# Hybrid decoder layer on one core: where seven big SBUF tiles begin, and which of their columns the up and down products use

## The chip, the cores and the metric

The kernel runs on one core of one Trainium2 chip. The metric is the time of one execution on the device in microseconds (us). Before the change it is 1274.11 us, the median of three runs (1274.04 to 1275.34).

## The reference, cut to what matters

One layer of a decoder over 1024 tokens and 16 meta tokens, model width 1024: an input projection, a convolution branch and a banded attention branch, both projected back and merged by gates, an output projection with a layer norm, and a feed-forward block of width 2816. The parts that the change touches are the last ones:

```
mixed = jax.nn.sigmoid(g_attn) * y_attn + jax.nn.sigmoid(g_conv) * y_conv
h = layer_norm(DEEPNORM_ALPHA * h + mixed @ w_out, ln1_g, ln1_b)
up = causal_dwconv(h @ ffn_w_up, ffn_dw, ffn_dw_b)
u, g = jnp.split(up, 2, axis=-1)
f = (jax.nn.gelu(g, approximate=False) * u) @ ffn_w_down
return layer_norm(DEEPNORM_ALPHA * h + f, ln2_g, ln2_b)
```

## The kernel before, in words

**Numbers in halves.** Each float32 operand of a large product is split into a high and a low part of type fp32r. A product is the sum of three: high by high, high by low, low by high. So matmuls come in threes, and each has a stationary operand of 128 columns of its own (loaded by LDWEIGHTS) and a moving operand of 256 to 512 columns. The code names the first operand of `nc.tensor.matmul` (after the output) the stationary one, the second the moving one.

**Stages.** The input projection (`ps_z`, L295 to L300, from operands in RHC and RHO), attention between its tiles, the two branch projections (`ps_p`, from OA and OC), the output projection (`ps_w`, `out_rows`, stationary pieces of the mixed rows in RHC and RHO, moving weights in OA, RX, RW and two small tiles), then up and down.

**Up** (L1480, the loop over 22 chunks `c`). Up is done as a Strassen product: seven products in place of eight. For each chunk there are seven stationary weight sums, and each is multiplied with one of seven sums of the rows, in two sub-blocks: sub-block 0 has 258 columns, sub-block 1 has 256. A product on one sub-block is 12 matmuls (four pieces of the contraction, three matmuls each), so a chunk has 7 x 2 x 12 = 168 matmuls, and the stage 3696. `B_AT` says in which tile and from which column each of the 14 row sums lies; a sum takes 4 x 258 x 2 = 2064 columns or 4 x 256 x 2 = 2048 columns, the four high pieces first and then the four low ones. The weights come from a ring of ten places of 1024 columns (`RING`): four in RHO from column 0, four in small tiles that the page names `ws`, and two in RHO from column 6160. Seven places are used in each chunk, so the ring turns against the seven products.

**Down** (L1613, `down`). Also seven products, each over 11 pieces taken in six pairs, four output rows of banks: 7 x 11 x 4 x 3 = 924 matmuls of 512 columns. The stationary operand (the activations) lies at the places of `F_AT`, six in turn; the moving one (the weights) at those of `W_DN`, seven in turn.

**Order.** Nothing in the order of the engines' work hangs on a byte address: the instructions are put in order by priorities (`rank`) and by `after`, and the tiles are placed by pools that stack from the left or the right end of SBUF. The built program of the changed kernel has the same instructions in the same order on every engine, queue for queue, with the same semaphore waits but for one value on DVE; only the addresses differ.

**Places in bytes.** In the built program FA, RHC, RHO and OB begin at a byte whose residue modulo 256 is 192, and so do the small weight tiles (`wr`, `whi`, `wlo`, `ws`). OA begins at residue 0, RX, RW and the two tiles of `sums` at 64, OC at 128. A column has 4 bytes, so 64 columns make 256 bytes.

Of the kernel before, what the change touches and what calls it, by code (L numbers as in the profile page):

```python
# [23 lines left out]
F = mybir.dt.float32  # L24
# [5 lines left out]
P = 128  # L30
# [71 lines left out]
def tile_hybrid_layer(  # L102
# [41 lines left out]
    RHC = arena.tile([P, 8320], R, name="RHC")  # L144
    RHO = arena.tile([P, 8320], R, name="RHO")
# [756 lines left out]
    late = ctx.enter_context(tc.tile_pool(name="late", bufs=1, side="right", reuse_waits="tile"))  # L902

    OC = late.tile([P, 8320], R, name="OC")
    late.tile([P, 24], F, name="pad_c")
    oa_stack = ExitStack()
    oa_p = oa_stack.enter_context(tc.tile_pool(name="oa", bufs=1, side="left", reuse_waits="tile"))
    oa_p.tile([P, 8], F, name="pad_a")
    OA = oa_p.tile([P, 8320], R, name="OA")
    tmp_stack = ExitStack()  # L910
    tmp_p = tmp_stack.enter_context(tc.tile_pool(name="tmp", bufs=1, side="right", reuse_waits="tile"))
# [104 lines left out]
    tmp_stack.close()  # L1016
    rx_p = ctx.enter_context(tc.tile_pool(name="rx", bufs=1, side="right", reuse_waits="tile"))
    RX = rx_p.tile([P, 2064], R, name="RX")
    wo_stack = ExitStack()
    RW = wo_stack.enter_context(tc.tile_pool(name="rw", bufs=1, side="right", reuse_waits="tile")).tile(  # L1020
        [P, 2048], R, name="RW")
# [22 lines left out]
    def prep_wo(k, raw=None, behind=None):  # L1044
        if k < 4:
            hi, lo = OA[:, k * 2048:k * 2048 + 1024], OA[:, k * 2048 + 1024:k * 2048 + 2048]
        elif k < 6:
            hi, lo = ((RX, RW)[k - 4][:, x:x + 1024] for x in (0, 1024))
        else:
# [83 lines left out]
    def quadrant(sub, kk, h):  # L1133
# [1 line left out]
        return FA[:, h1_at(sub, i):h1_at(sub, i + 4)]  # L1135


    B_AT = [[(RHC, 6256), (RHO, 4096), (OA, 0), (OA, 2064), (OA, 4128), (OA, 6192), (RX, 0)],
            [(OC, 0), (OC, 2048), (OC, 4096), (OC, 6144), (RHC, 112), (RHC, 2160), (RHC, 4208)]]
    B11, B21, BT2, BT1, BT3, BT4, B22 = range(7)  # L1140

    def bsum(sub, q, hl):
        n = SUB[sub][1] - SUB[sub][0]
        t, o = B_AT[sub][q]
        return t[:, o + hl * 4 * n:o + (hl + 1) * 4 * n]
# [141 lines left out]

    RING = [RHO[:, i * 1024:(i + 1) * 1024] for i in range(4)]
    RING += [None] * 4
    RING += [RHO[:, 6160 + i * 1024:6160 + (i + 1) * 1024] for i in range(2)]  # L1290
    ring_next = [0]

    def wsplit(src):
# [253 lines left out]
    T1, T3, T4, T2 = (blk(td, 0, 2048, q * 512) for q in range(4))  # L1547
    S2, S3, S4, S1 = (blk(sd, 0, 2048, q * 512) for q in range(4))

    F_AT = [(RHC, 6256), (RX, 0), (RHC, 2160), (RHO, 0), (RHO, 2048), (RHO, 4096)]  # L1550
    W_DN = [(OC, 0), (OC, 2048), (OC, 4096), (OC, 6144), (RHC, 112), (RHC, 4208), (RHO, 6144)]

    RXFs = [RXF[:, 0:1024], RXF[:, 1024:2048]]
    FAs = [FA[:, i * 1024:(i + 1) * 1024] for i in range(6)]
# [7 lines left out]
    def operand(i, src, j, n, raws, places):  # L1562
        raw = raws[i % len(raws)]
        if raw is None:
            raw = wraw([P, D])
        raw = raw[:, :n * 512]
        ins = load(raw.rearrange("p (n c) -> p n c", c=512), src(j, n))
        after(ins, loads[-1] if loads else f_stores[-5])
        loads.append(ins)
        t, o = places[i % len(places)]  # L1570
        hi, lo = (t[:, o + x:o + x + n * 512] for x in (0, 1024))
        nc.scalar.copy(hi, raw)
        los.append(nc.vector.tensor_tensor(lo, raw, f32(hi), OP.subtract))
        if len(los) > 1:
            after(los[-1], evacs.pop() if evacs else los[-2])
        return hi, lo

    def down_operands():
# [4 lines left out]
        for i, (f, w, j, n) in enumerate(x):  # L1583
            yield (n,) + operand(i, f, j, n, F_RAW, F_AT) + operand(i, w, j, n, W_RAW, W_DN)

# [181 lines left out]
```

## Time and profile before

| what | before |
|---|---|
| median of the runs | 1274.11 us |
| span of the profiled execution, first to last instruction | 1273.1 us |
| TensorE matmul (PE) busy | 1261.4 us, 8546 records |
| VectorE (DVE) busy | 1084.0 us |
| ScalarE (ACT) busy | 587.9 us |
| DMA, mean over the span | 167 GB/s |

The profiled execution itself took 1273.1 us by its instructions; the run times are about 1 us longer, with what lies ahead of the first instruction and behind the last one. A record of a matmul in the profile is longer than the matmul's turn on the engine: matmuls are pipelined, and one starts while the one before it still drains. So the time that a matmul takes of the stage is read from the distance between starts, and for a group of rows of the timeline it is the start of the next row less the start of this one, divided by the count. The second column of such a row is the time to the end of its last record.

### The profile page before, as it was taken

How to read it: one execution, taken by the hardware profiler on the slowest of the kernel's cores; microseconds unless marked ns; L12 is line 12 of the kernel's file. 1: busy time of each engine (PE TensorE's matmuls, PEld its weight loads, DVE VectorE, ACT ScalarE, POOL GpSimd, SP SyncE). 2: the span in 40 equal slices, each digit the busy share in tenths (PEclk: the TensorE clock that was granted, in tenths of full speed). 3: DMA queues.
4: the chain of work that ended last, by engine and by line, in shares of the span. 5: the costliest groups of instructions: out<-in, count | busy, mean ns of one | idle time of the engine just before them, and what ended most of it. 6: DMA issues, size and time to landing. Idle time of an engine off the chain costs nothing.

```text
span 1273.1 us, 21682 instructions
## 1 busy us (share of the span) xinstructions
PE 1261.4 (99%) x8546; PEld 1189.6 (93%) x8546; DVE 1084.0 (85%) x1837; ACT 587.9 (46%) x1066; POOL 53.1 (4%) x28
## 2 busy tenths in 40 slices
PE   9999999999999999999999999999999999999997
PEld 8999999999999999788899999999999998888885
DVE  7899989999999577548899999988989876996697
ACT  7522254645573232344655455455554544444330
POOL 0000000010112231000000000000000000000000
PEclk9999999999999999999999999999999999999999
DMA  7294633332256564222145546454454567988722
GB/s 275 74 306 106 184 93 99 102 95 84 68 152 177 158 165 117 83 90 76 67 158 200 190 168 214 158 207 145 156 196 161 202 225 284 387 317 310 247 83 83
DMA packets 96152, 212.10 MB, mean 167 GB/s; under 512 B 10787, under 2 KB 35939, under 8 KB 95922
## 3 DMA queue, kind: packets, MB, share of 16 engines
q1 hardware_dynamic: 84282, 199.64, 47.2%
q10 hardware_dynamic: 11768, 11.08, 2.7%
q8 instruction: 67, 1.10, 0.4%
q14 instruction: 35, 0.29, 0.1%
HBM read 150.29 MB, written 62.70 MB: 167 GB/s over the span
## 4 chain that ended last, share of the span: by engine, by line
PE 96%; DMA 2%; DVE 1%; ACT 0%; issue 0%; SPq 0%; DVEq 0%; ACTq 0%
PE px L1480 15%; PE ps_x L1613 10%; PE py L1480 10%; PE ps_z L299 7%; PE ps_z L295 7%; PE ps_z L300 7%; PE ps_z L1613 7%; PE pz L1480 5%; PE pw L1480 5%; PE ps_p L299 2%; PE ps_p L300 2%; PE ps_p L295 2%; PE ps_w L300 2%; PE ps_w L295 2%; PE ps_w L299 2%; PE ps_z L511 2%
## 5 line engine op out<-in xcount | busy, mean ns | idle before, releaser
L663 DVE SCALAR_TENSOR_TENSOR FA<-cin,cols,FA 128x1026 f32<-128x1026 f32 x120 | 155.1, 1303 | 0.2
L295 PE MATMUL ps_z<-RHO,whi 128*128 128x384 f32 (+2 forms) x324 | 104.8, 323 | 0.0
L299 PE MATMUL ps_z<-RHC,whi 128*128 128x384 f32 (+2 forms) x324 | 104.7, 323 | 0.0
L299 PE MATMUL ps_z<-RHO,whi 128*128 128x384 f32 (+2 forms) x324 | 104.0, 321 | 0.0
L295 PE MATMUL ps_z<-RHC,whi 128*128 128x384 f32 (+2 forms) x324 | 103.9, 321 | 0.0
L300 PE MATMUL ps_z<-RHC,wlo 128*128 128x384 f32 (+2 forms) x324 | 103.6, 320 | 0.0
L300 PE MATMUL ps_z<-RHO,wlo 128*128 128x384 f32 (+2 forms) x324 | 103.2, 319 | 0.0
L1302 DVE TENSOR_TENSOR RHO<-wr,RHO 128x512 fp32r<-128x512 f32 x94 | 63.4, 683 | 9.8 <-ACT RHO L1301 9.8
L1301 ACT CAST RHO<-wr 128x512 fp32r<-128x512 f32 x94 | 56.6, 619 | 26.4 <-DVE wr L1319 10.1
L266 ACT CAST whi<-wr 128x1024 fp32r<-128x1024 f32 x37 | 38.9, 1052 | 56.8 <-PE ps_z L299 36.7
L295 PEld LDWEIGHTS ps_z<-RHO,whi 128*128 128x128 f32 x324 | 60.9, 188 | 0.5 <-issue 0.3
L299 PEld LDWEIGHTS ps_z<-RHC,whi 128*128 128x128 f32 x324 | 60.9, 188 | 0.4
L300 PEld LDWEIGHTS ps_z<-RHC,wlo 128*128 128x128 f32 x324 | 61.0, 188 | 0.2
L300 PEld LDWEIGHTS ps_z<-RHO,wlo 128*128 128x128 f32 x324 | 60.9, 188 | 0.1
L295 PEld LDWEIGHTS ps_z<-RHC,whi 128*128 128x128 f32 x324 | 60.8, 188 | 0.2
L299 PEld LDWEIGHTS ps_z<-RHO,whi 128*128 128x128 f32 x324 | 60.9, 188 | 0.1
L1319 DVE TENSOR_TENSOR wr<-wr 128x512 f32<-128x512 f32 x88 | 60.0, 682 | 0.2
L269 POOL TENSOR_TENSOR wlo<-wr,whi 128x1024 fp32r<-128x1024 f32 x17 | 41.3, 2431 | 187.5 <-ACT whi L266 177.7
L1492 ACT COPY FA<-px 128x514 f32<-128x514 f32 (+2 forms) x23 | 13.2, 572 | 76.4 <-PE px L1480 76.4
L670 ACT ACTIVATE FA<-ps_z,cols 128x386 f32<-128x386 f32 (+2 forms) x48 | 26.0, 541 | 47.5 <-PE ps_z L300 43.0
L1302 DVE TENSOR_TENSOR ws<-wr,ws 128x512 fp32r<-128x512 f32 x60 | 40.6, 684 | 5.4 <-ACT ws L1301 5.3
L1480 PE MATMUL px<-OA,RHO 128*128 128x258 f32 x324 | 43.1, 282 | 0.0
(467 smaller groups left out, 3583.9 us busy)
## 6 DMA issues: line engine op xcount, KB each, us to landing
wr<-in_w_up_dram SPq DMA_DIRECT2D x44, 512.0 KB, 4.3
wr<-in_w_z_dram SPq DMA_DIRECT2D x30, 512.0 KB, 3.7
fd<-FA SPq DMA_DIRECT2D x44, 256.0 KB, 2.5
OB<-in_w_down_dram SPq DMA_DIRECT2D x19, 512.0 KB, 6.1
qt<-qd SPq DMA_DIRECT2D x28, 256.0 KB, 3.8
td<-OB SPq DMA_DIRECT2D x12, 512.0 KB, 3.5
sums<-fd SPq DMA_DIRECT2D x12, 512.0 KB
sd<-sums SPq DMA_DIRECT2D x12, 512.0 KB, 2.9
```

The costliest lines, as they stand in the source:

```text
L266: ins = nc.scalar.copy(hi, raw)
L269: return (nc.vector if quick else nc.gpsimd).tensor_tensor(lo, raw, f32(hi), OP.subtract)
L295: ins = nc.tensor.matmul(ps, ah, bh, start=i == 0, stop=False)
L299: nc.tensor.matmul(ps, ah, bl, start=False, stop=False)
L300: last = nc.tensor.matmul(ps, al, bh, start=False, stop=i == n - 1)
L663: nc.vector.scalar_tensor_tensor(acc[c], cin[:, j:j + U], wc, acc[c], OP.mult, OP.add)
L670: nc.scalar.activation(t, ps, AF.Tanh, bias=bcol(14 + i), scale=0.5)
L1301: nc.scalar.copy(hi, src)
L1302: ins = nc.vector.tensor_tensor(lo, src, f32(hi), OP.subtract)
L1319: ins = nc.vector.tensor_tensor(*x)
L1480: ins = nc.tensor.matmul(o, x[:, ks], bmat(sub, q, hl, k), start=first and k + j == 0, stop=k == 3 and j == 2, skip_group_check=not first)
L1613: nc.tensor.matmul(banks[i], l[:, ts], r[:, ws], start=first and a and x + k == 0, stop=z and x == len(ops) - 1 and k == 2, skip_group_che ...
```

## The change

It moves where tiles begin, by the size of three filler tiles (one of them new), and moves the columns that some operands take within their tiles. `late`, `oa` and `rx` are pools; `pad_c`, `pad_a` and `pad_x` are never read or written.

```
     OC = late.tile([P, 8320], R, name="OC")
-    late.tile([P, 24], F, name="pad_c")
+    late.tile([P, 8], F, name="pad_c")
...
-    oa_p.tile([P, 8], F, name="pad_a")
+    oa_p.tile([P, 56], F, name="pad_a")
     OA = oa_p.tile([P, 8320], R, name="OA")
...
     RX = rx_p.tile([P, 2064], R, name="RX")
+    rx_p.tile([P, 48], F, name="pad_x")
...
-    B_AT = [[(RHC, 6256), (RHO, 4096), (OA, 0), (OA, 2064), (OA, 4128), (OA, 6192), (RX, 0)],
-            [(OC, 0), (OC, 2048), (OC, 4096), (OC, 6144), (RHC, 112), (RHC, 2160), (RHC, 4208)]]
+    B_AT = [[(RHC, 6208), (RHO, 4096), (OA, 0), (OA, 2064), (OA, 4128), (OA, 6208), (RX, 0)],
+            [(OC, 16), (OC, 2064), (OC, 4112), (OC, 6160), (RHC, 2064), (RHC, 16), (RHC, 4112)]]
     B11, B21, BT2, BT1, BT3, BT4, B22 = range(7)
...
-    RING += [RHO[:, 6160 + i * 1024:6160 + (i + 1) * 1024] for i in range(2)]
+    RING += [RHO[:, 6208 + i * 1024:6208 + (i + 1) * 1024] for i in range(2)]
...
-    F_AT = [(RHC, 6256), (RX, 0), (RHC, 2160), (RHO, 0), (RHO, 2048), (RHO, 4096)]
-    W_DN = [(OC, 0), (OC, 2048), (OC, 4096), (OC, 6144), (RHC, 112), (RHC, 4208), (RHO, 6144)]
+    F_AT = [(RHC, 6208), (RX, 0), (RHC, 0), (RHO, 0), (RHO, 2048), (RHO, 4096)]
+    W_DN = [(OC, 0), (OC, 2048), (OC, 4096), (OC, 6144), (RHC, 2048), (RHC, 4096), (RHO, 6144)]
```

In the built program of the changed kernel FA, RHC, RHO, OB, OA, OC and RX all begin at residue 192 (RW and the two tiles of `sums` too). The residues of the first bytes of the operands, before and after:

| operand | before | after |
|---|---|---|
| up, stationary: ring places | 192 (eight places), 0 (two) | 192 (all ten) |
| up, moving, sub-block 1 (256 columns) | 128 (all seven) | 0 (all seven) |
| up, moving, sub-block 0 (258 columns): B11, B21, BT2, BT1, BT3, BT4, B22 | 128, 192, 0, 64, 128, 192, 64 | 192, 192, 192, 0, 64, 192, 192 |
| down, stationary (`F_AT`) | 128, 64, 128, 192, 192, 192 | 192 (all six) |
| down, moving (`W_DN`) | 128 (six places), 192 (one) | 192 (all seven) |

In sub-block 0 each of the four pieces lies 258 columns behind the one before it, so its residue is 8 more, and the low pieces lie 32 further; this is the same before and after.

## Prediction

> **What bounds the kernel now.** I read the page first, then the time of each engine by stage (the windows), then the timeline of PE, row by row.
>
> ```profile
> span 1273.1 us, 21682 instructions
> PE 1261.4 (99%) x8546; PEld 1189.6 (93%) x8546; DVE 1084.0 (85%) x1837; ACT 587.9 (46%) x1066; POOL 53.1 (4%) x28
> PE 96%; DMA 2%; DVE 1%; ACT 0%; issue 0%; SPq 0%; DVEq 0%; ACTq 0%
> 634.00:1051.80 417.80, 417.80 (x3542) 417.80 (x3541) 377.78 (x604) 219.30 (x361) 0.00 (x0) 1.00 0.52 183
> 1051.80:1265.20 213.40, 213.32 (x926) 173.36 (x925) 169.68 (x239) 82.03 (x92) 0.00 (x0) 1.00 0.69 247
> ```
>
> The first three lines are from the page: PE is busy for 99% of the span, and 96% of the chain that ended last is PE. The last two are windows: the stretch, its length, then busy time and count of PE, weight load, DVE, ACT and POOL, granted clock, DMA share and GB/s. Nearly all of up (634 to 1051.8) and all of down (1051.8 to 1265.2) run without an idle PE at full granted clock. So the time of these 631 us is the number of matmuls times the distance between their starts, and that distance is what I looked at. In up it is 417.80 / 3542 = 118.0 ns on average. The change leaves all instructions, their order and their waits alone and changes addresses; whether it does anything is whether the distance between starts depends on addresses. It does, and the timeline of down shows it:
>
> ```profile
> 1057.31 5.66 PE L1613 MATMUL ps_z<-OC,RX 128*128 128x512 f32 x24
> 1062.80 5.60 PE L1613 MATMUL ps_z<-OC,RHC 128*128 128x512 f32 x24
> 1068.24 5.76 PE L1613 MATMUL ps_z<-OC,RHO 128*128 128x512 f32 x24
> 1073.84 5.76 PE L1613 MATMUL ps_z<-RHC,RHO 128*128 128x512 f32 x24
> 1079.44 2.93 PE L1613 MATMUL ps_z<-RHO,RHC 128*128 128x512 f32 x12
> ...
> 1190.33 5.64 PE L1613 MATMUL ps_x<-RHO 128*128 128x512 f32 x24
> 1195.81 8.56 PE L1613 MATMUL ps_x<-OC,RHO 128*128 128x512 f32 x36
> ```
>
> These are the same 24 matmuls of 512 columns each time, with no idle time between, and only the places differ. Let the **distance** be the residue of the moving operand less that of the stationary one, modulo 256 bytes. OC with RHC (column 2160) is 128 and 128, distance 0: 1068.24 - 1062.80 = 5.44 us, 226.7 ns each. OC with RX is 128 and 64, distance 64: 5.49 us, 228.8 ns. OC or RHC with RHO is 128 and 192, distance 192: 5.60 us twice, 233.3 ns. That it is the distance and not the residue itself, the row at 1190.33 shows: both in RHO, 192 and 192, distance 0 again: 5.48 us, 228.3 ns, with a first few matmuls that settle after another distance.
>
> The Trainium skill, SBUF — State Buffer, section "Who interferes with whom", says that PE never waits on anyone, and TensorE: Matmul & The Clock Gate, section "Step-by-step: what each phase is for", that loading the next weights does not take read bandwidth from the running matmul. By that rule no placing would change the time; the trace disagrees, 5.44 against 5.60 us for equal work. The rule's result is kept as a rival below.
>
> **Part 1: down (F_AT, W_DN, the bases).** Going through the 42 pairs of down, 348 of the 924 matmuls stand at distance 0, 180 at 64, 24 at 128 and 372 at 192. Afterwards all 924 stand at 0.
>
> ```profile
> 1052.01 30.36 PE ps_z L1613 x132
> 1082.37 30.66 PE ps_x L1613 x132
> 1113.03 30.53 PE ps_z L1613 x132
> 1143.55 60.83 PE ps_x L1613 x264
> 1204.38 30.29 PE ps_z L1613 x132
> 1234.66 30.48 PE ps_x L1613 x132
> ```
>
> The chain in order of time gives the stage: 30.36 + 30.66 + 30.53 + 60.83 + 30.29 + 30.48 = 213.15 us. At 226.7 ns each, 924 take 209.5. I leave 0.1 us for settling at the start (the row at 1190.33 cost 0.04 us): **-3.6 us**. Bounds: -3.7, and -1.7 if distance 0 settles anew in each pair as at 1190.33 (228.3 ns). This part is the surest, because both kinds of row at distance 0 are in the trace. DVE (169.68 of 213.40 us) and DMA (share 0.69) supply the operands with time to spare, and PE did not wait for them; if that cover went, PE would idle up to the 3.6 us that it gained.
>
> **Part 2: up, sub-block 1 (256 columns, 1848 matmuls).** One round of seven products, sub-block 0 and 1 in turn:
>
> ```profile
> 699.22 1.58 PE L1480 MATMUL pz<-OC,RHO 128*128 128x256 f32 x12
> 700.64 1.60 PE L1480 MATMUL px<-OA,RHO 128*128 128x258 f32 x12
> 702.08 1.52 PE L1480 MATMUL px<-OC,RHO 128*128 128x256 f32 x12
> 703.44 1.63 PE L1480 MATMUL pw<-OA,RHO 128*128 128x258 f32 x12
> 704.91 1.53 PE L1480 MATMUL pw<-RHC,RHO 128*128 128x256 f32 x12
> 706.28 1.61 PE L1480 MATMUL py<-OA,RHO 128*128 128x258 f32 x12
> 707.73 1.54 PE L1480 MATMUL py<-OC,RHO 128*128 128x256 f32 x12
> 709.11 1.60 PE L1480 MATMUL px<-OA,RHO 128*128 128x258 f32 x12
> 710.54 1.58 PE L1480 MATMUL px<-RHC,RHO 128*128 128x256 f32 x12
> 711.95 1.62 PE L1480 MATMUL py<-RX,ws 128*128 128x258 f32 x12
> 713.41 1.53 PE L1480 MATMUL py<-RHC,ws 128*128 128x256 f32 x12
> 714.77 1.60 PE L1480 MATMUL px<-RHC,ws 128*128 128x258 f32 x12
> 716.20 1.58 PE L1480 MATMUL px<-OC,ws 128*128 128x256 f32 x12
> 717.62 1.58 PE L1480 MATMUL pz<-RHO,ws 128*128 128x258 f32 x12
> 719.04 1.52 PE L1480 MATMUL pz<-OC,ws 128*128 128x256 f32 x12
> 720.40 0.88 PE L1480 MATMUL px<-OA,RHO 128*128 128x258 f32 x6
> ```
>
> Starts subtracted, the seven 256-column rows from 702.08 on take 1.36, 1.37, 1.38, 1.41, 1.36, 1.42 and 1.36 us: 113.3 ns each in a fast step, 118 ns in a slow one, at one and the same distance (128 less 192, so 192). So here the distance does not settle it alone; the phase in which the product before hands over does as well. The row at 699.22 has its weights in a ring place of residue 0, distance 128: 1.42 us, 118.3 ns. With eight ring places of ten at 192 the mean is 0.8 x 115.0 + 0.2 x 118.3 = 115.7; summing the starts of all 1848 gives 116.1, which I use.
>
> Afterwards all 1848 stand at distance 64 (0 less 192), and no row of up shows that. Bounds: 113.3 ns, the fast step held throughout, -5.2 us; 118.3 ns, a slow step throughout, +4.1 us. Between them I go by the nearest row, distance 64 in down, which costs 228.8 - 226.7 = 2.1 ns over the best one: 113.3 + 2.1 = 115.4 ns, (116.1 - 115.4) x 1848 = 1.3 us. I take **-1.0 us**. Going over to one ring residue is in this sum.
>
> **Part 3: up, sub-block 0 (258 columns, 1848 matmuls).** The seven rows take 1.44, 1.47, 1.45, 1.43, 1.46, 1.43 and 1.42 us, in the mean 120.2 ns. Five of the seven move to distance 0 (1320 matmuls), BT1 to 64, BT3 to 128. Two rows have distance 0 already: 717.62 (RHO, 1.42 us, 118.3 ns) and 703.44 (OA at 192, 1.47 us, 122.5 ns), the cheapest and the dearest of the round; their mean, 120.4, is the mean of all. I take **0**, with bounds of 1320 x 1.9 ns = -2.5 us and 1320 x 2.3 ns = +3.0 us.
>
> **Part 4: output and branch projections.**
>
> ```profile
> 506.29 0.39 PE L295 MATMUL ps_w<-RX,RHC 128*128 128x512 f32 x1
> ...
> 510.93 0.39 PE L299 MATMUL ps_w<-OA,RHC 128*128 128x512 f32 x1
> 511.16 0.28 PE L295 MATMUL ps_p<-OC,whi 128*128 128x256 f32 x1
> ```
>
> From 506.29 to 511.16 stand 21 matmuls of 512 columns, 231.9 ns each, at distances 64 (OA) and 128 (RX, RW). Afterwards they stand at 0. Of the 384 such matmuls some 290 have their weights in OA, RX or RW; at 226.7 they would gain up to 290 x 5.2 ns = 1.5 us, but transposes cut each row's products into short runs that settle anew. I take **-0.8 us**, bounds 0 and -1.5. The branch projections read OA and OC with residues that step by 64 and 128 from matmul to matmul, so a new base turns the same cycle: 0. Everything ahead of them keeps its addresses. The tail behind the last matmul is DVE and DMA work on tiles that keep theirs.
>
> **The sum.** -3.6 - 1.0 + 0 - 0.8 = -5.4 us on the profiled 1273.1 us. Run times lie 1.0 us above that span, and nothing outside it changes: 1274.1 - 5.4 = **1268.7 us**. DVE is busy for 377.78 of 417.80 us in up and has room for the 1 us by which up gets shorter.
>
> **Rivals.**
> - Up settles in the fast step: 113.3 ns in sub-block 1 and 118.3 in the five products at distance 0, a further -4.2 - 2.5 us: 1262.0; half of it, 1265. For it: one stationary residue, one moving residue, nothing that disturbs the phase from chunk to chunk. Against it: the 258-column pieces still step by 8 bytes, so each handover differs. Chance 0.18.
> - No placing counts (the rule of the two pages), or what the rows show comes from the tiles and not from residues: 1274.1. Against it stand the rows at distance 0 in two different pairs of tiles. Chance 0.07.
> - What down gains, up gives back: a slow step throughout in sub-block 1, -3.6 - 0.8 + 4.1 = -0.3 us: 1273.8. Chance 0.13.
> - Slower: the phase in which a product starts. Distance 64 leaves each 256-column product at 118.3 ns and hands every following product at distance 0 over into the dear form of the row at 703.44: +4.1 + 3.0 - 1.7 (down settling in each pair) - 0 = +5.4 us: 1279.5. It decides against the change once a matmul of up costs 1.2 ns more than now (4.4 us / 3696). Chance 0.06.
>
> **How the numbers follow.** The forecast case (0.56) covers 1266.0 to 1271.5 with the bounds of parts 2 and 3 half used. A difference of 0.2%, 2.5 us, is about what a measurement of this kernel can tell from none; faster means below 1271.6. Forecast and first rival are faster, 0.74, the second, third and a little of the forecast's upper edge are the same, 0.20, slower 0.06. The range reaches over half of the first rival and to the two unchanged ones: 1264.0 to 1274.2.
>
> **What would show it.** Down: every 24 matmuls 5.44 us, the whole 209.5 us. Up: rows of 256 columns at 1.36 to 1.42 us, all seven alike in their distance; a mean below 1.38 us confirms part 2, 1.42 refutes it. The forecast is wrong if down's rows keep 5.49 to 5.60 us, or if the mean over up leaves 117 to 118.2 ns.

## The result and the profile after

The changed kernel takes 1270.92 us (median of eight runs, 1270.74 to 1271.21), the kernel before beside it 1274.22 us (median of eight, 1274.04 to 1275.34). The ratio is 0.9972 with a 95% interval of 0.9962 to 0.9982: 3.3 us faster, and the interval, 2.3 to 4.8 us, does not reach to no difference. The forecast was 1268.7 us; the time lies in its range, 2.2 us above its point.

From the page of the kernel after (span; busy time of each engine; the chain that ended last by engine), and below it the two windows in the columns of before:

```profile
span 1268.5 us, 21682 instructions
PE 1257.3 (99%) x8546; PEld 1190.5 (94%) x8546; DVE 1084.0 (85%) x1837; ACT 588.3 (46%) x1066; POOL 53.1 (4%) x28
PE 98%; DVE 1%; ACT 0%; DMA 0%; issue 0%; SPq 0%; DVEq 0%
```

```profile
634.00:1051.80 417.80, 417.80 (x3534) 417.66 (x3533) 377.65 (x602) 219.49 (x360) 0.00 (x0) 1.00 0.51 184
1051.80:1265.20 213.40, 208.73 (x921) 172.49 (x919) 173.18 (x247) 81.51 (x92) 0.00 (x0) 1.00 0.69 249
```

PE is still busy for 99% of the span, from 634 us on without an idle moment in up and at full granted clock. So the distance between starts still decides the time of these stages. (The changed kernel has one line more, so L1480 and L1613 of before are L1481 and L1614 here.) The second window ends behind the last matmul now, hence 208.73 of 213.40 us.

Which stage gave what is read from the first start of each stage. The profile shown of before belongs to the longest of its runs (1275.34 us), so the comparison is with a second one of the same kernel (run b2_before, below). Its timeline, at the first branch projection, the first product of up and the first of down:

```profile
416.23 0.28 PE L295 MATMUL ps_p<-OA,whi 128*128 128x258 f32 x1
...
611.33 1.58 PE L1480 MATMUL px<-OC,RHO 128*128 128x256 f32 x12
...
1050.66 1.09 PE L1613 MATMUL ps_z<-OC,RHC 128*128 128x512 f32 x4
```

The same three of the kernel after:

```profile
416.40 0.28 PE L295 MATMUL ps_p<-OA,whi 128*128 128x258 f32 x1
...
611.18 1.58 PE L1481 MATMUL px<-OC,RHO 128*128 128x256 f32 x12
...
1050.90 0.85 PE L1614 MATMUL ps_z<-OC,RHC 128*128 128x512 f32 x3
```

| stage | before, second profile | after | difference | forecast |
|---|---|---|---|---|
| ahead of the branch projections | 416.23 | 416.40 | +0.2 | 0 |
| branch and output projections | 195.10 | 194.78 | -0.3 | -0.8 |
| up | 439.33 | 439.72 | +0.4 | -1.0 |
| down and tail, to the end of the span (1271.9, 1268.5) | 221.2 | 217.6 | -3.6 | -3.6 |

The net gain is down's, and down's is what was forecast to a tenth; the other stages nearly cancel. The chain of waits shows down in the same pieces as before:

```profile
1051.07 29.95 PE ps_z L1614 x132
1081.01 29.92 PE ps_x L1614 x132
1110.93 29.92 PE ps_z L1614 x132
```

132 matmuls take 29.92 us a piece, 226.7 ns each, where before they took 30.29 to 30.66, and the same holds for the pieces that follow. No pair settles anew.

Four products of a round of up in the timeline after, with the start of the next one behind each pair, to be laid beside the round shown of before:

```profile
702.06 1.58 PE L1481 MATMUL pw<-OA,RHO 128*128 128x258 f32 x12
703.48 1.57 PE L1481 MATMUL pw<-RHC,RHO 128*128 128x256 f32 x12
704.89 1.60 PE L1481 MATMUL py<-OA,RHO 128*128 128x258 f32 x12
...
710.61 1.59 PE L1481 MATMUL py<-RX,ws 128*128 128x258 f32 x12
712.04 1.52 PE L1481 MATMUL py<-RHC,ws 128*128 128x256 f32 x12
713.40 1.60 PE L1481 MATMUL px<-RHC,ws 128*128 128x258 f32 x12
```

The 258-column rows, both at distance 0, take 1.42 and 1.43 us. Of the two 256-column rows, both at distance 64, BT4 (703.48) takes 1.41 us, 118 ns a matmul, and B22 (712.04) 1.36 us, 113.3 ns. The first chunk does all of sub-block 1 ahead of sub-block 0; in the 21 chunks behind it, six of the seven products of sub-block 1 take 117.6 to 118.1 ns and B22 takes 113.3. Over all starts of the stage the mean goes from 116.10 to **117.18 ns**. In sub-block 0 three of the five products at distance 0 take 118.3 ns in these 21 chunks, the other two 119.0 (B22) and 119.8 (B11, behind the quick part of B22); the mean over all goes from 120.03 to **119.24 ns**. Up as a whole is 0.4 us longer.

### The profile page after: what moved, and what is told of

The parts are those of the page before. It is cut to its first block, busy times and chain, and to the rows that moved or that the text cites. A ratio compares the mean times of both kernels' runs of the same rounds, so it can differ in the third digit from the quotient of the medians.

```text
span 1268.5 us, 21682 instructions
## 1 busy us (share of the span) xinstructions
PE 1257.3 (99%) x8546; PEld 1190.5 (94%) x8546; DVE 1084.0 (85%) x1837; ACT 588.3 (46%) x1066; POOL 53.1 (4%) x28
## 4 chain that ended last, share of the span: by engine, by line
PE 98%; DVE 1%; ACT 0%; DMA 0%; issue 0%; SPq 0%; DVEq 0%
PE px L1481 15%; PE py L1481 10%; PE ps_x L1614 9%; PE ps_z L299 8%; PE ps_z L295 8%; PE ps_z L300 8%; PE ps_z L1614 7%; PE pw L1481 5%; PE pz L1481 5%; PE ps_p L299 2%; PE ps_p L295 2%; PE ps_p L300 2%; PE ps_w L295 2%; PE ps_w L300 2%; PE ps_w L299 2%; PE ps_z L511 2%
## 5 line engine op out<-in xcount | busy, mean ns | idle before, releaser
L1481 PE MATMUL px<-OA,RHO 128*128 128x258 f32 x324 | 43.3, 282 | 0.0
```

Of the source, the lines that this page charges most:

```text
L1481: ins = nc.tensor.matmul(o, x[:, ks], bmat(sub, q, hl, k), start=first and k + j == 0, stop=k == 3 and j == 2, skip_group_check=not first)
```

## The experiments

Each is an edit of the changed kernel, but the last. "Distance" is used as in the prediction. The "step" of a matmul is the distance in time from its start to the next one. The theory was that a matmul's step is set by its distance, and within up also by the phase in which the product before hands over (theory A in the expectations); the rivals were that the distance alone sets it (B), that residues do not count in up (C), and that the residue or the tile does. The ratio given is to the kernel before, run beside each experiment. The difference from the kernel after is taken between medians, 1270.92 us for it; since the kernel before took 1274.6 to 1274.8 us beside the experiments and 1274.22 beside the kernel after, a difference of half a microsecond between them says nothing. The means per matmul are over all starts of a stage with no wait between; ranges over products leave out the first chunk.

**Sub-block 1 at distance 0 (e1_up_d0).**

```
-            [(OC, 16), (OC, 2064), (OC, 4112), (OC, 6160), (RHC, 2064), (RHC, 16), (RHC, 4112)]]
+            [(OC, 0), (OC, 2048), (OC, 4096), (OC, 6144), (RHC, 2048), (RHC, 0), (RHC, 4096)]]
```

> The changed kernel with the moving operands of up's sub-block 1 at residue 192, so that they stand at distance 0 from the weights (changed kernel: 64). Theory A, the distance and the phase handed over by the product before set which step a whole product of 12 keeps: each product takes a fast step (1.36 us) or a slow one (1.41 us), all 12 alike; at distance 0 the fast one is as likely as in down, so sub-block 1 falls from 117.2 to between 113.3 and 116 ns and the time from 1270.9 to between 1263.7 and 1268.7 us. Theory B, the distance alone sets the step: 113.3 ns for every product, 1263.7 us. Theory C, residues do not count in up (up stayed as it was under the change): 1270.9 us.

1276.60 us, ratio to before 1.0014 (1.0005 to 1.0024). The timeline:

```profile
702.02 1.60 PE L1481 MATMUL px<-OC,RHO 128*128 128x256 f32 x12
703.46 1.60 PE L1481 MATMUL pw<-OA,RHO 128*128 128x258 f32 x12
```

The 256-column row takes 1.44 us, and so do six of the seven: after two quicker starts each of them runs at 120.0 ns, 119.3 in the mean of all. Sub-block 0, which nothing touched, goes from 119.24 to 120.03 ns. All three theories missed. The distance that is the best for 512 columns is the worst of the four for 256, so the price measured in down could not be carried to up.

**Sub-block 1 at distance 192 (e2_up_d192).** The same line with 48 in place of 16 columns:

```
+            [(OC, 48), (OC, 2096), (OC, 4144), (OC, 6192), (RHC, 2096), (RHC, 48), (RHC, 4144)]]
```

> The changed kernel with sub-block 1 of up at residue 128, distance 192, as in most products of the kernel before. A: the handover decides, and at this distance five of seven products were fast before, so about 115 ns in place of 117.2, 1267 us; bounds 113.3 ns (1263.7) and 118 ns (1272.4). B: distance 192 is the dearest in down (6.6 ns over the best), so 118 to 120 ns in every product, 1272.4 to 1276. C: 1270.9.

1270.51 us, 0.9967 (0.9955 to 0.9979).

```profile
700.90 1.53 PE L1481 MATMUL px<-OC,RHO 128*128 128x256 f32 x12
702.27 1.63 PE L1481 MATMUL pw<-OA,RHO 128*128 128x258 f32 x12
703.74 1.53 PE L1481 MATMUL pw<-RHC,RHO 128*128 128x256 f32 x12
705.11 1.60 PE L1481 MATMUL py<-OA,RHO 128*128 128x258 f32 x12
```

Now the 256-column rows take 1.37 us (114.29 ns in the mean), but the 258-column rows, which nothing touched, take 1.47 us (702.27 to 703.74) where they took 1.42 in the kernel after. All products of sub-block 0 at distance 0 rise to 122.2 to 122.4 ns. Sub-block 1 gains 2.9 ns x 1848 = 5.3 us, sub-block 0 loses (121.63 - 119.24) x 1848 = 4.4 us. The time alone, 0.4 us from the kernel after, would fit theory C; the rows show that two changes cancelled in it. Theory A is within its bounds, but had priced sub-block 1 alone; B is out. A product whose own places stay is dearer by 4 ns a matmul because its neighbours moved. That it is the one ahead that counts, and not the one behind, e10 shows below.

**Sub-block 1 at distance 128 (e3_up_d128).** With 32 columns:

```
+            [(OC, 32), (OC, 2080), (OC, 4128), (OC, 6176), (RHC, 2080), (RHC, 32), (RHC, 4128)]]
```

> The changed kernel with sub-block 1 of up at residue 64, distance 128. The rows of the kernel before at this distance (ring places of residue 0) took 118.3 to 119.7 ns and never settled in one step. A and B: 118.3 to 119.7 ns in every product, 1272.9 to 1275.5 us. C: 1270.9.

1274.13 us, 0.9996 (0.9986 to 1.0005). Sub-block 1 takes 118.91 ns, sub-block 0 119.19. As A and B expected; C is out.

**Down at distance 192, from the moving side (e4_down_mov) and from the stationary side (e5_down_sta).**

```
-    W_DN = [(OC, 0), (OC, 2048), (OC, 4096), (OC, 6144), (RHC, 2048), (RHC, 4096), (RHO, 6144)]
+    W_DN = [(OC, 48), (OC, 2096), (OC, 4144), (OC, 6192), (RHC, 2096), (RHC, 4144), (RHO, 6192)]
```

```
-    F_AT = [(RHC, 6208), (RX, 0), (RHC, 0), (RHO, 0), (RHO, 2048), (RHO, 4096)]
-    W_DN = [(OC, 0), (OC, 2048), (OC, 4096), (OC, 6144), (RHC, 2048), (RHC, 4096), (RHO, 6144)]
+    F_AT = [(RHC, 6224), (RX, 16), (RHC, 16), (RHO, 16), (RHO, 2064), (RHO, 4112)]
+    W_DN = [(OC, 0), (OC, 2048), (OC, 4096), (OC, 6144), (RHC, 2112), (RHC, 4160), (RHO, 6208)]
```

> The changed kernel with the moving operands of down (W_DN) 48 columns further, so at residue 128 and distance 192 in all 924 matmuls. A and B: 233.3 ns each, 215.6 us for down in place of 209.6, so 1270.9 + 6.1 = 1277.0 us; up as in the changed kernel. If not the distance but the traffic of the other engines had set the step of down: 209.6 us, 1270.9.

> The changed kernel with the stationary operands of down (F_AT) 16 columns further, at residue 0, so that all 924 matmuls stand at distance 192 again, but with the moving operands where the change has them (192). The distance decides: 233.3 ns each and 1277 us, as when the moving ones were moved. The residue of the moving operand decides: 226.7 ns and 1270.9 us.

One run each: 1277.23 and 1277.63 us. First e4, then e5, in the timeline:

```profile
1062.45 5.76 PE L1614 MATMUL ps_z<-OC,RHC 128*128 128x512 f32 x24
1068.05 5.76 PE L1614 MATMUL ps_z<-OC,RHO 128*128 128x512 f32 x24
```

```profile
1062.80 5.76 PE L1614 MATMUL ps_z<-OC,RHC 128*128 128x512 f32 x24
1068.40 5.76 PE L1614 MATMUL ps_z<-OC,RHO 128*128 128x512 f32 x24
```

24 matmuls take 5.60 us in both, 233.3 ns each, with the moving operand at residue 128 in e4 and still at 192 in e5 (three of its places move there by 64 columns, which are 256 bytes). Down takes 215.75 us in both profiles, 6.1 us more than the 209.63 of the kernel after; the times are 6.3 and 6.7 us longer. So neither the residue of one operand nor the tile sets the step of down, but the distance.

**Everything 32 bytes further, all distances kept (e6_shift).**

```
+    const.tile([P, 8], F, name="pad_0")
...
-    late.tile([P, 8], F, name="pad_c")
```

> The changed kernel with everything 32 bytes further: every tile from the first one on and OC, RX, RW, all now at residue 224, all distances as they were. If only distances count: the same gaps in every product, 1270.9 us within 0.6. If the residue itself counts (an operand that begins 32 bytes into a block of 64): gaps in down other than 226.7 ns, and a time off by several us.

1271.18 us, 0.9973 (0.9962 to 0.9983): the time of the kernel after, as expected if only distances count. In the profile sub-block 1 takes 117.18 ns, sub-block 0 119.23 and down 209.63 us, all as in the kernel after. At residue 224 the placing is worth what it is at 192; what the run keeps is the distances.

**The branch projections (e7_proj).** Their rows move by 14 columns, so that the 256-column pieces stand at multiples of 64 bytes from their weights.

```
-        o = (c * 2 + hl) * T
+        o = (c * 2 + hl) * T + 14
...
-        o = (r * 2 + hl) * T
+        o = (r * 2 + hl) * T + 14
```

> The changed kernel with the operands of the branch projections 14 columns further in OA and OC, so that the pieces of 256 columns begin at a multiple of 64 bytes (now 8 bytes past one) and stand in the cycle of distances that they had before the change. Theory: distance and start inside a 64-byte block set the gap; 121.1 ns now, 120.0 in the kernel before, 117.7 for the aligned pieces of 256 columns of the input projection, so 576 x 3.4 ns = 2.0 us less, 1268.9. If only the cycle of distances counts: 120.0 ns, 0.7 us less, 1270.2. If neither: 1270.9.

1269.81 us, 0.9961 (0.9946 to 0.9976), 1.1 below the kernel after. The first matmul of 256 columns and the one 24 places on, in the kernel before (second profile), the kernel after and e7:

```profile
419.09 0.28 PE L295 MATMUL ps_p<-OA,whi 128*128 128x256 f32 x1
...
421.96 0.28 PE L295 MATMUL ps_p<-OA,whi 128*128 128x256 f32 x1
```

```profile
419.31 0.29 PE L295 MATMUL ps_p<-OA,whi 128*128 128x256 f32 x1
...
422.22 0.29 PE L295 MATMUL ps_p<-OA,whi 128*128 128x256 f32 x1
```

```profile
419.80 0.28 PE L295 MATMUL ps_p<-OA,whi 128*128 128x256 f32 x1
...
422.65 0.28 PE L295 MATMUL ps_p<-OA,whi 128*128 128x256 f32 x1
```

The 24 matmuls take 2.87 us before, 2.91 after and 2.85 in e7. Over all 768 the branch projections take 92.06, 92.95 and 91.71 us: the change cost 0.9 us here, and e7 takes 1.2 back. That lies between the two expectations, 2.0 and 0.7 us: the pieces of 256 columns take 118.9 ns, where 117.7 and 120.0 were expected. The run changed the cycle of distances and the start inside 64 bytes together, so how much of the gain belongs to either stays open.

**Both sub-blocks of up moved (e8_pairs).** Sub-block 1 at distance 192 as in e2, and sub-block 0 off distance 0: five products at 64, two at 128.

```
-    RX = rx_p.tile([P, 2064], R, name="RX")
-    rx_p.tile([P, 48], F, name="pad_x")
+    RX = rx_p.tile([P, 2080], R, name="RX")
+    rx_p.tile([P, 32], F, name="pad_x")
...
+    B_AT = [[(RHC, 6224), (RHO, 4112), (OA, 16), (OA, 2080), (OA, 4176), (OA, 6240), (RX, 16)],
+            [(OC, 48), (OC, 2096), (OC, 4144), (OC, 6192), (RHC, 2096), (RHC, 48), (RHC, 4144)]]
```

> Up placed by the table that the runs so far give for a sub-block 0 product and the sub-block 1 product behind it: sub-block 1 at distance 192 (fast step 113.3 ns), sub-block 0 at distance 64 in five products and 128 in two (BT1, BT4). Handover theory: entered from the fast step, the pair takes 119.4 + 113.3 ns at 64 and 120.9 + 114.7 at 128, so (5 x 232.7 + 2 x 235.6) / 7 = 233.5 ns a pair against 236.4 in the changed kernel: 1848 x 2.9 ns = 5.4 us less, 1265.5 us. Each product by its distance alone (mean of what its distance showed so far, 119.5 and 120.7 in sub-block 0, 114.3 in sub-block 1): 234.2, 4.1 us less, 1266.8. If the gain of distance 192 is given back in sub-block 0 as in the run with distance 192 and the old places: 1270.5.

1265.86 us, 0.9930 (0.9914 to 0.9947): faster than both kernels, and 0.4 us from what the handover theory gave. The two other expectations, 0.9 and 4.6 us off, fit less well; between the first two the time alone hardly decides.

```profile
708.18 1.52 PE L1481 MATMUL px<-RHC,RHO 128*128 128x256 f32 x12
709.54 1.60 PE L1481 MATMUL py<-RX,ws 128*128 128x258 f32 x12
710.97 1.52 PE L1481 MATMUL py<-RHC,ws 128*128 128x256 f32 x12
712.33 1.60 PE L1481 MATMUL px<-RHC,ws 128*128 128x258 f32 x12
```

1.36, 1.43, 1.36 us: the quick step of sub-block 1 stays (113.82 ns in the mean) and sub-block 0 pays 119.86 ns for it instead of e2's 121.63. Product by product it is 119.5 and 113.3 ns at distance 64, 120.9 and 114.7 at 128, as the handover theory had it from e2.

**e7 and e8 together (e9_both).** RX and `pad_x` are as in e8 too.

```
+        o = (c * 2 + hl) * T + 14
...
+        o = (r * 2 + hl) * T + 14
...
+    B_AT = [[(RHC, 6224), (RHO, 4112), (OA, 16), (OA, 2080), (OA, 4176), (OA, 6240), (RX, 16)],
+            [(OC, 48), (OC, 2096), (OC, 4144), (OC, 6192), (RHC, 2096), (RHC, 48), (RHC, 4144)]]
```

> Puts the places of e8 (up) and of e7 (branch projections) together. Theory A, each stage pays by its own distances and by what the product before hands over, and the stages are independent: e8's 1265.9 us less e7's gain of 1.1 us = 1264.8 us, with the branch projections at 91.7 us and up at 434.9. Rival: e7's gain lay in the front part of its run and not in the projections: 1265.9 us. Slower than 1265.9: up's pattern depends on the phase in which the projections leave the engine.

1264.89 us, 0.9924 (0.9911 to 0.9936), span 1262.5 us: as expected, the best of all. The branch projections take 91.71 us in it. Its timeline at the first product of up and of down:

```profile
609.85 1.58 PE L1481 MATMUL px<-OC,RHO 128*128 128x256 f32 x12
...
1044.94 5.62 PE L1614 MATMUL ps_z<-OC,RHC 128*128 128x512 f32 x24
```

Up takes 435.09 us, 4.6 less than in the kernel after and within 0.2 us of e8's. The stages add up; what the projections hand on matters no more than that to up.

**Sub-block 0 at distance 192 (e10_s0_192).** Against e8 (RX grows to 2112 columns in place of `pad_x`):

```
-    B_AT = [[(RHC, 6224), (RHO, 4112), (OA, 16), (OA, 2080), (OA, 4176), (OA, 6240), (RX, 16)],
+    B_AT = [[(RHC, 6256), (RHO, 4144), (OA, 48), (OA, 2112), (OA, 4176), (OA, 6256), (RX, 48)],
```

> As e8, but sub-block 0 of up moves on by 32 columns: five of its products to distance 192, BT1 to 0, BT3 to 64; sub-block 1 stays at 192. Theory A (a product of 258 columns costs by its own distance and by the step it is entered from, and no simple order of the distances holds): bounds from e8's 119.5 ns (1265.9 us) and e2's 122.3 ns (1270.5 us) a matmul; no value between them is favoured. Rival (the distance that is best for 256 columns is best for 258 too): 118 ns or less, 1263.6 us.

1270.96 us, 0.9971 (0.9960 to 0.9982), half a microsecond above the upper bound that was given, and not for the reason that stood behind that bound.

```profile
703.58 1.58 PE L1480 MATMUL pw<-RHC,RHO 128*128 128x256 f32 x12
705.00 1.58 PE L1480 MATMUL py<-OA,RHO 128*128 128x258 f32 x12
706.42 1.52 PE L1480 MATMUL py<-OC,RHO 128*128 128x256 f32 x12
707.78 1.60 PE L1480 MATMUL px<-OA,RHO 128*128 128x258 f32 x12
709.21 1.52 PE L1480 MATMUL px<-RHC,RHO 128*128 128x256 f32 x12
```

Sub-block 0 costs 119.52 ns, at the lower bound. But sub-block 1, whose places are those of e8, is slow again: 1.42 us (703.58) behind each product at distance 192, 118.0 ns in all five of them, and 1.36 us (706.42, 709.21) behind the two at distances 0 and 64. The handover works in this direction too, and I had priced only the other one. It is the product ahead that decides: the quick BT3 is followed by a product at distance 192, as are four of the five that take 118.0 ns, and BT4, which takes 118.0, is followed by one at distance 0.

**The products ahead of a 256-column product at distance 64 (e11_entry).** Sub-block 1 as in the kernel after, sub-block 0, RX and `pad_x` as in e8.

```
-    B_AT = [[(RHC, 6208), (RHO, 4096), (OA, 0), (OA, 2064), (OA, 4128), (OA, 6208), (RX, 0)],
+    B_AT = [[(RHC, 6224), (RHO, 4112), (OA, 16), (OA, 2080), (OA, 4176), (OA, 6240), (RX, 16)],
```

> Sub-block 1 of up stays as in the changed kernel (distance 64, 117.8 ns in six products and 113.3 in B22); only the products ahead of it move: sub-block 0 goes from distance 0 to 64 (five products) and from 64 and 128 to 128 (two). Handover theory (at distance 64 too the step is chosen by the product before, and it is distance 0 before it that brings the slow step): sub-block 1 falls to 113.3 ns in most products, 1848 x 3.9 ns = 7.2 us less, sub-block 0 costs 119.9 ns as in e8, 1.2 us more: 1264.9 us. Rival (distance 64 has a price of its own for 256 columns and B22 was the exception): sub-block 1 stays at 117.8 ns: 1272.1 us. Between them, two products of seven fast: 1270.

1273.63 us, 0.9992 (0.9982 to 1.0001).

```profile
713.18 1.57 PE L1481 MATMUL py<-RHC,ws 128*128 128x256 f32 x12
714.60 1.60 PE L1481 MATMUL px<-RHC,ws 128*128 128x258 f32 x12
```

All seven products take 117.7 to 118.1 ns, B22 (713.18, 1.42 us) now among them. My theory that distance 0 ahead had spoilt them falls; at distance 64 the slow step is the rule behind distances 0, 64 and 128, and the one quick product was the exception. That one, B22 in the kernel after, has distance 0 ahead of it, like four of the products that take 118 ns, so the pair does not settle the step either; why it was quick stays open. The time lies 1.5 us above the rival's 1272.1: 117.80 - 117.18 ns is another 1.1 us, since the exception went too, and the rest is too little to read.

**The kernel before again (b2_before).** No edit.

> The kernel before once more, for a second profile. If the run time is always the span and 2.27 us, and the first profile was of one of the longer runs: a span of about 1272.0 us at a time of 1274.2, with up at 439.7, down at 213.3 and the projections at 195.1 us as in the first, and the difference ahead of the first projection. Rival: the stages themselves vary from run to run by tenths of a microsecond.

1274.17 us.

```profile
span 1271.9 us, 21682 instructions
```

Run time less span is 2.3 us, as in the kernel after (1270.77 and 1268.5). The first profile began its branch projections and up 0.87 us later:

```profile
417.10 0.28 PE L295 MATMUL ps_p<-OA,whi 128*128 128x258 f32 x1
...
612.20 0.99 PE L1480 MATMUL px<-OC,RHO 128*128 128x256 f32 x7
```

The projections take 195.10 us in both. So 0.87 of the 1.2 us between the two spans lie ahead of them, and the rest is in up (439.65 us there, 439.33 here), at its start: at one wait of PE near 624 us two starts lie 0.80 us apart there and 0.41 here. Over the whole of up the means of the two profiles agree within 0.1 ns, and down takes 213.28 us in both. So the expectation holds but for up, which varies by tenths as the rival had it.

But single products do not. In the first chunk, product BT3 of sub-block 1 in the first profile and in the second:

```profile
621.49 1.52 PE L1480 MATMUL px<-RHC,ws 128*128 128x256 f32 x12
622.85 1.64 PE L1480 MATMUL py<-RHC,ws 128*128 128x256 f32 x12
```

```profile
620.70 1.58 PE L1480 MATMUL px<-RHC,ws 128*128 128x256 f32 x12
622.11 1.58 PE L1480 MATMUL py<-RHC,ws 128*128 128x256 f32 x12
```

1.36 us against 1.41: 113.3 and 117.7 ns a matmul in the same kernel, at the same addresses and with the same products ahead, since the last wait of PE (0.98 us in both). So at distance 192 a product can hold either step, and addresses alone, its own and those ahead, do not choose between them. Something finer in the time at which PE sets off again may; no run isolates it.

## Why the prediction came out as it did

The point was 2.2 us too low. Part by part, with the means of the second profile of before and of the kernel after:

| part | forecast | measured | how |
|---|---|---|---|
| 1, down | -3.6 | -3.65 | 213.28 to 209.63 us, first start to last end |
| 2, up, sub-block 1 | -1.0 | **+2.0** | (117.18 - 116.10) x 1848 |
| 3, up, sub-block 0 | 0 | -1.5 | (119.24 - 120.03) x 1848 |
| 4, output projection | -0.8 | -1.2 | 93.95 to 92.75 us, starts summed |
| 4, branch projections | 0 | **+0.9** | 92.06 to 92.95 us |
| ahead of the projections; wait near 623 us | 0 | 0.0 | +0.2 and -0.1, which vary from run to run |
| sum | -5.4 | -3.4 | spans 1271.9 to 1268.5 |

- **Down was right** in mechanism and size. That one distance throughout sets the step there, e4 and e5 show from both sides and e6 shows for all tiles at once. The rival "no placing counts" is out: the same 924 matmuls take 6.1 us more when only the distance goes from 0 to 192. The Trainium skill, SBUF — State Buffer, section "Who interferes with whom", says that PE never waits on anyone. The prediction read from this that no placing would count, and that does not hold here: 226.7 against 233.3 ns with nothing else changed. What, if anything, PE waits for there no run shows.
- **Part 2 is the step that failed.** It took 115.4 ns for a 256-column matmul at distance 64, "the nearest row, distance 64 in down", plus 2.1 ns over the best step. Measured is 117.18, 1.8 ns more: 3.3 us, or 3.0 of the sum, since 0.3 of the gain had been rounded off. The working carried a price from 512 to 256 columns. e1 and e2 show how wrong that is: distance 0, the best there (226.7 ns), is the worst here (119.3), and distance 192, the dearest measured there, the best here (114.3). Even for 512 columns the price was that of one row among others: further on in the same stage of the kernel before, a pair at distance 64 (OC, RX) that follows distance 192 takes 5.60 us, 233.3 ns a matmul, and keeps that step to its end.

```profile
1087.80 5.76 PE L1613 MATMUL ps_x<-OC,RX 128*128 128x512 f32 x24
1093.40 5.62 PE L1613 MATMUL ps_x<-OC,RHC 128*128 128x512 f32 x24
```

  So what ran ahead counts in down too, where distances alternate. The row that should have counted for part 2 was at hand: up's own rows ran at distance 192 with a quick step, and the change took all of them off it. The bounds, 113.3 and 118.3, held. By the prediction's own signs part 2 is neither confirmed nor refuted (rows of 1.41 us in the mean, between 1.38 and 1.42), and the mean over up, 118.2 ns, lies at the edge of what it allowed.
- **Part 3 was too cautious.** It took the mean of a cheap and a dear row for distance 0. Which of the two it would be hangs on the product ahead: 118.3 ns in three products of the kernel after, behind sub-block 1 at distance 64 and 117.6 to 117.8 ns, and 122.2 to 122.4 in e2, behind sub-block 1 at distance 192 and 114.3 ns. So the two errors belong together and leave up at +0.5 us, before its one wait near 623 us. A rule "slow ahead makes cheap" does not follow: in e1 products at distance 0 take 120.1 ns behind 119.4, in e3 B22 takes 121.6 behind 118.3, and in the kernel after B11 takes 119.8 behind 113.3.
- **Part 4.** The output projection gained more than forecast. The forecast halved the gain because short runs would settle anew; this one does not lose by it: 20 matmuls of the kernel after, the last of its run, take 540.21 to 544.74, 226.5 ns each.

```profile
540.21 0.39 PE L295 MATMUL ps_w<-RW,RHC 128*128 128x512 f32 x1
...
544.74 0.40 PE L300 MATMUL ps_w<-whi,RHC 128*128 128x512 f32 x1
```

  The sentence on the branch projections, "a new base turns the same cycle: 0", is wrong on its own terms. By the built programs, of the 576 matmuls of 256 columns 96, 192, 96 and 192 stand at distances 8, 72, 136 and 200 before, and 192, 96, 192 and 96 after. The cycle has the same members in other shares. e7 moves each of them by 56 bytes, which gives the shares of before at 0, 64, 128 and 192, and takes 1.2 us off.
- **Span and run time.** "Run times lie 1.0 us above that span" compared a profile of one run with the median of others. Each run lies 2.3 us above its own span; the first profile was of a run 1.2 us longer than the median. Since the sum was taken off the median, this did not shift the forecast.
- **The rivals.** "What down gains, up gives back" was half true: sub-block 1 took the slow step in six of seven products, but sub-block 0 made most of it good. "Fast step throughout" did not come at distance 64; e8 shows that the quick step can be held, at distance 192: 5.1 us below the kernel after and 2.8 below the forecast. "Slower" did not come: the dear form of sub-block 0 came in e2, behind the quick step of sub-block 1, not behind the slow one.

What stays open is what in the chip makes the step. In down one distance throughout gives one step, 226.7 or 233.3 ns; where distances alternate, what ran ahead counts as well. In up the runs show cases and no rule: e10 and e11 show that I could not yet forecast a new pair of distances, and the two profiles of the kernel before show one product at two steps.

## What to carry to other kernels

When PE has no idle time, measure the step between matmul starts for each pair of operands, not only the count of matmuls; equal work differed by 3% (512 columns) and 5% (256 columns) here through the places of its operands alone. A price read at one width did not hold at another, and a product's price depended on the one ahead of it, so choose the places of neighbouring products together and try them. Compare a profile with its own run's time before laying it beside a median.

## What the runs showed of the hardware that was not expected

The mean step in ns of a product with operands of type fp32r, by distance in bytes (512 columns from down; the others from up in the kernel after and the experiments, each value the mean of one product over the 21 chunks behind the first; for 258 columns the distance is that of the first piece):

| distance | 512 columns | 256 columns | 258 columns |
|---|---|---|---|
| 0 | 226.7 | 118.7 to 119.4 | 118.2 to 122.4, by what ran ahead |
| 64 | 228 to 230 in the kernel before, once 233.3 behind distance 192 | 117.6 to 118.1, once 113.3 | 118.4 to 119.7 |
| 128 | not measured alone | 118.3 to 119.1 | 119.6 to 121.3 |
| 192 | 233.3 | 113.3 to 114.7, or 118.0 behind 258 columns at 192 | 119.4 to 119.9 |

The steps are regular. At distance 0 the matmuls of down start 226 or 227 ns apart one after the other, 226.7 in the mean; at distance 192 they alternate between about 231 and 236 ns, 233.3 in the mean. The quick step of 256 columns is a row of 113 and 114 ns, and the 117.8 ns of distance 64 is a repeating mixture of 117 to 119. In the kernel after, the mean of a product lies within 0.1 ns of its usual value in nearly all of the 21 chunks behind the first. Why the steps have these lengths no run here tells.
